# Three banks in rotation for transposes and PV, scores of the heads apart in quarter one, norm weights folded into the rounding

## The chip, the cores and the metric

The kernel runs on one core of a Trainium2 chip. The metric is the device time of one execution in microseconds (us), median of three runs. The core has these engines: PE or TensorE (matrix products and transposes), DVE or VectorE, ACT or ScalarE, POOL or GpSimd, and SP, which here only issues transfers. Each works through its own queue in order. Products land in PSUM, eight banks of 128 partitions by 512 float32 values.

## The reference

One layer of a transformer trunk in float32: 2048 tokens, width 1024, 16 heads of 64, a feed-forward of width 2816. With depth 1 it is:

```
h = rms_norm(x, g_pre_mix)
q, k, v = heads of h @ w_qkv
for chunk c (64 queries): keys of chunks max(0, c-8) .. c
    p = softmax(q @ k.T / 8 + bias[relative position, clipped])
    o = p @ v
x = x + rms_norm(o @ w_o, g_post_mix)
h = rms_norm(x, g_pre_ffn)
x = x + rms_norm((silu(h @ w_gate) * (h @ w_up)) @ w_down, g_post_ffn)
```

rms_norm divides by the root of the mean square of a token and multiplies by a weight for each column.

## The kernel before

**Products.** A float32 product is made of rounded parts: an operand is split into a high part (rounded by ScalarE) and a low part (the rest, a VectorE subtraction; `split`, L352). `products` (L195) makes three matmuls of it, high by high, high by low, low by high (L197, L198, L199). The large products of the projections and of the feed-forward also work on sums and differences of quarter matrices in the way of Strassen, so an operand comes in columns named B11, B21, T1, T2, B22, T4, T3. `Blocks.build` makes these columns from four raw loads (L11, L21, L12, L22), and `put` splits each.

**Order.** TensorE runs its instructions in program order (a manual schedule, L1509). The other engines' instructions are ordered by the compiler's scheduler. Work that is not TensorE's main line stands in a queue `later` as pairs (cost, step); `tick(w)` is called with each triple of matmuls (a unit, some 0.68 us), and it runs steps as their costs are covered. `pause(w)` is a step that only waits; `timed` sets steps to given units.

**Stages.** First the projections: `project` (L1277) goes through two groups of 1024 tokens. In each, values come first (`values_of`), then queries and keys (`queries_keys`), with one product for each column name; after each, a callback `after(name)` queues the columns of group two into buffers that have become free. The roots of the norms come through `roots` and `roots_by_tokens` (L1311), whose argument `back` is the pause before the root is spread. Group one ends at about 275 us, group two at about 498.

Then attention, in four quarters of 512 tokens in the order n = 1, 0, 2, 3 (`SEQ_OF`), each with 8 jobs (two heads by 512 queries) of four steps (128 queries each). The step, in program order:

```
[each fourth step: half the fill, then output() of the job before]
job.transposed(t % 4)          # head 0: 4 transposes, DVE copy L551; head 1: 4, ACT copy L553
scaled() of step t + 2         # DVE reciprocal L530, POOL scaling L533
scores of step t + 3           # 8 matmuls L508, L509; per head DVE L517 (bias, minimum), ACT exp L521
[each fourth step: low(), the DVE subtraction L585 that reads po]
half the fill
job.fifth()                    # 2 transposes L562, ACT copy L563
half the fill
```

`output` (L584) is PV, 32 matmuls into one bank (16 to 20 for n = 0), an ACT eviction L584 and the subtraction `low`. The fill is the output projection of the quarter before (`o_quarter`), so quarter one has none. For n = 0 there are fewer key blocks and no fifth. PSUM: `st`, one tile of three banks, holds the scores of both heads; for n = 0 head 0 stands in its first bank and head 1 in its second (`cuts`, `(0, n), (512, 512 + n)`), else the heads follow each other and share the middle bank. `tt` has two buffers of one bank, `po` one bank, and the pool `ps` two (tag `mm`) for the fill and the rest.

After the attention the last output projection (1103 to 1145 us) runs while the feed-forward's first columns are loaded and built (`first`, L1630 on), and then the feed-forward to the end.

Of the kernel before, what the change touches and what calls it, by code (L numbers as in the profile page):

```python
# [49 lines left out]
def trunk(  # L50
# [393 lines left out]

    class Attend:


        def __init__(self, n, p):
            self.n, self.p = n, p
            self.prev = n > 0  # L450
            self.sc = {}
            self.pT = None

# [37 lines left out]
        def scores(self, ib):  # L491
# [9 lines left out]
            if "S" not in phase:  # L501
                phase["S"] = phase["psa"].tile([P, 3 * HALF], F32, name="st", bufs=1)
            st = phase["S"]
# [33 lines left out]
        def transposed(self, ib):  # L537
# [6 lines left out]
            for h in range(2):  # L544
                part = blocks[:4]
                tt = phase["psa"].tile([P, 4, P], F32, tag="tt", name="tt", bufs=2)
                for u, (r, b) in enumerate(part):
                    pe.transpose(tt[:, u, :], sc[h][:, b * P : b * P + P], ident)  # L548
                dst = self.pT[:, h, 0 : len(part), cols]
                if h == 0:  # L550
                    dve.tensor_copy(dst, tt[:, : len(part), :])  # L551
                else:
                    act.activation(dst, tt[:, : len(part), :], AF.Copy)  # L553
            self.rest = (sc, blocks[4], cols) if self.prev else None

        def fifth(self):
            if self.rest is None:
                return
            sc, (r, b), cols = self.rest
            tt = phase["psa"].tile([P, 4, P], F32, tag="tt", name="tt", bufs=2)  # L560
            for h in range(2):
                pe.transpose(tt[:, h, :], sc[h][:, b * P : b * P + P], ident)  # L562
            act.activation(self.pT[:, :, 4, cols], tt[:, 0:2, :], AF.Copy)  # L563

        def output(self):
# [8 lines left out]
            po = phase["psa"].tile([P, HALF], F32, tag="po", name="po", bufs=1)  # L574
# [36 lines left out]
    class Blocks:  # L611
# [53 lines left out]
        def put(self, name, k, src):  # L665
            if name not in self.t:
                self.t[name] = hb_tile(self.slot[name])
            split(self.t[name][:, 0, k, :], self.t[name][:, 1, k, :], src)

        def build(self, part, w, prep):  # L670
# [17 lines left out]

            def b11(k):
                prep(0, k, at("T3", 1, k))  # L690
                self.put("B11", k, at("T3", 1, k))

            def b21(k):
                prep(0, k + 4, at("T4", 1, k))
                self.put("B21", k, at("T4", 1, k))

            def t1(k):
# [3 lines left out]
                self.put("T1", k, a)  # L701

            def t2(k):
# [3 lines left out]
                dve.tensor_tensor(a, c, a, op=ALU.add)  # L707
                self.put("T2", k, a)
                dve.tensor_tensor(b, b, c, op=ALU.subtract)
                dve.tensor_tensor(a, d, a, op=ALU.subtract)  # L710
# [566 lines left out]
    def project():  # L1277

        warm = ps.tile([P, HALF], F32, tag="mm", name="warm")
        for _ in range(28):  # L1280
# [7 lines left out]
        def prepare(g):  # L1288
            def prep(t, k, x_):
# [4 lines left out]
                act.activation(x_, x_, AF.Copy, scale=gt[:, PRE_MIX, k : k + 1])  # L1294
# [3 lines left out]
        def build(g, part, w=0.0):  # L1298
            return groups[g].build(part, w, prepare(g))
# [48 lines left out]
        for k, (_, f) in enumerate(build(0, "B11")):  # L1348
# [6 lines left out]
            (1.0, build(0, "B21", 2.5)), (14.0, build(0, "T1", 3.5)[:1]), (17.0, roots(0, 2.0)),  # L1355
            (20.0, build(0, "T1", 3.0)[1:]), (30.0, build(0, "T2", 3.5)), (45.0, roots_by_tokens(1, 0.5, 2.0, spare)),
# [3 lines left out]
        for g in range(NG):  # L1360
# [7 lines left out]
            def after(name, g=g):  # L1368
# [10 lines left out]
                elif name == "T2":  # L1379
                    later.extend(timed((0.5, build(1, "B21", 1.8))))  # L1380
                elif name == "B22":
                    later.extend(timed((0.5, build(1, "T1", 1.8))))
                elif name == "T3":
                    later.extend(timed((0.5, build(1, "T2", 3.0))))
                elif name == "T4":
                    later.extend(timed(
                        (20.0, build(1, "B22", 3.0)), (34.0, build(1, "T4", 3.0)), (50.0, build(1, "T3", 2.0)),
# [206 lines left out]
    for part in ("L11", "L21", "L12", "L22"):  # L1594
        first(part, 0.0)[0][1]()
    later.extend(blocks[0].spreads() + timed(
# [80 lines left out]
```

## Time and profile before

| | |
|---|---|
| median of 3 runs | 2446.71 us (2444.43 to 2447.67) |
| profiled execution | 2446.41 us |
| its span | 2444.6 us |
| TensorE busy | 2347.2 us, 96% |
| VectorE, ScalarE, GpSimd busy | 1644.1, 1163.2, 316.7 us |
| mean granted TensorE clock | 0.991 of full speed |

The rows of the profile are read as: start and length, or busy time, then engine, line (L12 is line 12 of the kernel), operation, output and input by the program's names, shapes, and in square brackets how long the engine stood idle before and what released it. PEld is TensorE's weight load. Matmul lengths overlap in the pipeline, so distances between starts are used for what a matmul costs.

### The profile page before, as it was taken

Reading aid. Unit: us, or ns where it says so; the run is one execution under the profiler, and the core shown is the slowest. Engines: PE = TensorE matmul, PEld = TensorE weight load, DVE = VectorE, ACT = ScalarE, POOL = GpSimd, SP = SyncE. Lnnn points to the kernel's source line nnn. Section 1 sums busy time; section 2 is a strip of 40 time slices with the busy share of each in tenths; the row PEclk is TensorE's granted clock in tenths of the full one; section 3 lists DMA queues with packets and bytes.
Section 4 is the critical chain, followed back from the end, with each engine's and each line's share of the span. In section 5 each row is a group of like instructions: output and inputs, shape, how many; then the busy total and the mean of one; then the engine's idle time right before and its main releaser. Section 6 shows DMA issues by size and latency. Waiting matters only on the chain.

```text
span 2444.6 us, 33016 instructions
## 1 busy us (share of the span) xinstructions
PE 2347.2 (96%) x11480; PEld 1903.1 (78%) x11480; DVE 1644.1 (67%) x2625; ACT 1163.2 (48%) x2039; POOL 316.7 (13%) x422
## 2 busy tenths in 40 slices
PE   8999899989999899998999999999999999999998
PEld 6887688866676676767887888888888888888887
DVE  7775856666665556667876777677657667555567
ACT  8443733357665555664433333365433333334454
POOL 1012110023334324330000000000000000000002
PEclk9999999999999999999999999999999999999999
DMA  7699997678798878946666544287666757446654
GB/s 281 215 293 311 306 274 233 186 208 226 198 230 234 261 207 227 246 139 235 230 210 238 194 173 167 101 268 240 213 219 202 235 158 239 137 169 233 193 187 153
DMA packets 229782, 529.72 MB, mean 217 GB/s; under 512 B 26320, under 2 KB 42720, under 8 KB 225136
## 3 DMA queue, kind: packets, MB, share of 16 engines
q1 hardware_dynamic: 217712, 480.42, 62.6%
q0 software_dynamic: 11904, 47.19, 6.5%
q8 instruction: 91, 1.49, 0.3%
q14 instruction: 75, 0.61, 0.1%
HBM read 380.14 MB, written 170.44 MB: 225 GB/s over the span
## 4 chain that ended last, share of the span: by engine, by line
PE 54%; DVE 2%; issue 2%; DMA 1%; ACT 1%; POOL 0%; SPq 0%; DVEq 0%; ACTq 0%; POOLq 0%
PE pd L199 6%; PE pd L198 6%; PE pd L197 6%; PE pb L197 4%; PE pb L199 4%; PE pb L198 4%; PE pc L199 3%; PE pc L198 3%; PE pc L197 3%; PE pa L198 3%; PE pa L199 3%; PE pa L197 3%; PE po L578 1%; PE mm L199 1%; PE mm L197 1%
## 5 line engine op out<-in xcount | busy, mean ns | idle before, releaser
L533 POOL TENSOR_SCALAR sc<-sc,rows 128x640 f32<-128x640 f32 (+4 forms) x256 | 195.6, 777 | 364.7 <-DVE rows L530 221.9
L521 ACT ACTIVATE sc<-sc,rows 128x640 f32<-128x640 f32 (+4 forms) x256 | 192.9, 755 | 88.6 <-DVE rows L517 88.1
L517 DVE CUSTOM_DVE_ANT_0 sc<-st,bias 128x640 f32<-128x640 f32 (+2 forms) x248 | 173.6, 734 | 57.0 <-PE st L509 31.9
L197 PE MATMUL pb<-hb,w_wg_T 128*128 128x512 f32 x528 | 206.4, 391 | 3.8 <-DVE terms L966 3.8
L199 PE MATMUL pb<-hb,w_wg_T 128*128 128x512 f32 x528 | 206.2, 391 | 0.0
L198 PE MATMUL pb<-hb,w_wg_T 128*128 128x512 f32 x528 | 206.1, 390 | 0.0
L548 PE MATMUL tt<-ident,sc 128*128 128x128 f32 x928 | 135.0, 278 | 34.3 <-DVE pT L551 10.2
L548 PEld LDWEIGHTS tt<-ident,sc 128*128 128x128 f32 x928 | 105.1, 141 | 76.9 <-issue 45.0
L508 PE MATMUL st<-k,q 128*128 128x384 f32 (+3 forms) x432 | 137.4, 338 | 14.4 <-DVE rows L517 13.1
L199 PE MATMUL pd<-a,w_d_T 128*128 128x512 f32 (+1 forms) x368 | 139.9, 380 | 0.1
L197 PE MATMUL pd<-a,w_d_T 128*128 128x512 f32 (+1 forms) x368 | 139.9, 380 | 0.0
L198 PE MATMUL pd<-a,w_d_T 128*128 128x512 f32 (+1 forms) x368 | 139.8, 380 | 0.0
L551 DVE COPY pT<-tt 128x512 f32<-128x512 f32 (+3 forms) x128 | 81.5, 637 | 83.7 <-PE tt L548 63.6
L198 PE MATMUL pa<-hb,w_wg_B 128*128 128x512 f32 x352 | 136.9, 389 | 0.0
L197 PE MATMUL pa<-hb,w_wg_B 128*128 128x512 f32 x352 | 136.9, 389 | 0.0
L199 PE MATMUL pa<-hb,w_wg_B 128*128 128x512 f32 x352 | 136.9, 389 | 0.0
L968 ACT ACTIVATE terms<-terms 128x512 f32<-128x512 f32 x65 | 41.1, 632 | 182.5 <-DVE terms L966 182.5
L131 ACT ACTIVATE w_wg_T<-raw 128x1024 fp32r<-128x1024 f32 x88 | 92.9, 1057 | 71.9 <-PE pa L199 35.1
L509 PE MATMUL st<-k,q 128*128 128x384 f32 (+3 forms) x432 | 126.9, 314 | 0.0
L354 DVE TENSOR_TENSOR a<-raw_a,a 128x512 fp32r<-128x512 f32 x154 | 105.5, 692 | 25.2 <-ACT a L353 24.8
L289 POOL TENSOR_TENSOR rs<-ms,neg_half 128x4 f32<-128x4 f32 (+1 forms) x7 | 8.4, 1201 | 863.9 <-DVE ms L287 863.9
L197 PEld LDWEIGHTS pb<-hb,w_wg_T 128*128 128x128 f32 x528 | 99.5, 188 | 25.8 <-issue 4.6
(265 smaller groups left out, 6248.9 us busy)
## 6 DMA issues: line engine op xcount, KB each, us to landing
raw<-in_w_gu SPq DMA_DIRECT2D x77, 512.0 KB, 4.2
q<-q SPq DMA_DIRECT2D x62, 512.0 KB, 6.7
k<-k SPq DMA_DIRECT2D x54, 512.0 KB, 9.0
s_g_S<-raw POOLq DMA_DIRECT2D x44, 512.0 KB, 3.0
raw_d<-d_S SPq DMA_DIRECT2D x88, 256.0 KB, 3.6
raw_a<-aT SPq DMA_DIRECT2D x88, 256.0 KB, 3.5
raw<-s_g_S SPq DMA_DIRECT2D x44, 512.0 KB, 4.2
bias<-ext_d SPq DMA_DIRECT2D x124, 144.0 KB, 9.0
```

What stands on the lines that cost most here:

```text
L131: act.activation(hi, raw, AF.Copy)
L197: pe.matmul(pt, a_hi, b_hi, start=first, stop=False, skip_group_check=go_on)
L198: pe.matmul(pt, a_hi, b_lo, start=False, stop=False, skip_group_check=go_on)
L199: pe.matmul(pt, a_lo, b_hi, start=False, stop=last, skip_group_check=go_on)
L354: eng.tensor_tensor(lo, src, hi.bitcast(F32), op=ALU.subtract)
L508: pe.matmul(st[:, a:b], q[:, 2 * h, cols], kk[:, h, key], start=True, stop=False)
L509: pe.matmul(st[:, a:b], q[:, 2 * h + 1, cols], kk[:, h, key], start=False, stop=True)
L517: dve.tensor_tensor_reduce(out=sc[:, :n], in0=st[:, c0 : c0 + n], in1=rev, scale=-1.0, scalar=3.0e38, op0=ALU.add, op1=ALU.min, accum_out= ...
L521: act.activation(sc[:, :n], sc[:, :n], AF.Exp, bias=nmax, scale=-1.0, accum_out=rows[:, h : h + 1])
L533: last_pool[0] = pool.tensor_scalar(sc[:, :n], sc[:, :n], rows[:, 2 + h : 3 + h], 1.0, op0=ALU.mult, op1=ALU.mult)
L548: pe.transpose(tt[:, u, :], sc[h][:, b * P : b * P + P], ident)
L551: dve.tensor_copy(dst, tt[:, : len(part), :])
```

## The change

Attention: one PSUM tile of six banks, `banks`, takes the place of `st`, `tt` and `po`. In quarters two to four the scores keep banks 0 to 2, and transposes, fifth transposes and PV take banks 3, 4, 5 in turn. In quarter one (`alone`) head 0's scores stand in banks 0 and 1, head 1's in 2 and 3, the fifth in 4, PV in 5, and the first transposes in the two `mm` buffers of the pool `ps`, which no fill uses there.

Projections: `prepare` no longer multiplies each raw column by the norm weight on ScalarE. With `lazy`, `put` gives the weight as scale to the rounding (ScalarE) and to the subtraction (VectorE); T2's two other results take it in their VectorE operation, and one of its inputs by a ScalarE copy. In B11 and B21 the square for the norm's sum comes after the split. The warm-up matmuls go from 28 to 20, the pauses before the spreads of roots 0 and 1 from 2 to 14 and from 2 to 8 units. Group two's B21 columns are queued after B22 rather than T2, and T1 and T2 after T4, with the later ones set back.

Feed-forward: `fetch()`, which issues the loads of the next weights, is called after the first of four raw loads.

```
--- before.py
+++ after.py
@@ -442,14 +442,33 @@
             for h, own in enumerate(heads):
                 sp.dma_start(k_d[n][p][heads[a], h, :], part[own])
 
+    turn_of = [0]
+
+    def banks():
+        if "banks" not in phase:
+            phase["banks"] = phase["psa"].tile([P, 6 * HALF], F32, name="banks", bufs=1)
+        return phase["banks"]
+
     class Attend:
 
 
         def __init__(self, n, p):
             self.n, self.p = n, p
             self.prev = n > 0
+            self.alone = n == SEQ_OF[0]
             self.sc = {}
             self.pT = None
+
+        def bank(self, name):
+
+            if self.alone and name != "t5":
+                return ps.tile([P, HALF], F32, tag="mm", name="tt")
+            if self.alone:
+                at = 4
+            else:
+                at = 3 + turn_of[0] % 3
+                turn_of[0] += 1
+            return banks()[:, at * HALF : at * HALF + HALF]
 
         def load(self, begin=False):
             n, p, ap = self.n, self.p, phase.get("ap")
@@ -498,9 +517,9 @@
             else:
                 n, k0 = (ib + 1) * P, HALF
                 cuts = [(0, n), (512, 512 + n)]
-            if "S" not in phase:
-                phase["S"] = phase["psa"].tile([P, 3 * HALF], F32, name="st", bufs=1)
-            st = phase["S"]
+            st = banks()
+            if self.alone:
+                cuts = [(0, 512, 640), (1024, 1536, 1664)]
             for h in range(2):
                 c0 = cuts[h][0]
                 for a, b in zip(cuts[h][:-1], cuts[h][1:]):
@@ -543,7 +562,7 @@
             blocks = self.blocks(ib)
             for h in range(2):
                 part = blocks[:4]
-                tt = phase["psa"].tile([P, 4, P], F32, tag="tt", name="tt", bufs=2)
+                tt = self.bank("tt").rearrange("p (a b) -> p a b", a=4)
                 for u, (r, b) in enumerate(part):
                     pe.transpose(tt[:, u, :], sc[h][:, b * P : b * P + P], ident)
                 dst = self.pT[:, h, 0 : len(part), cols]
@@ -557,7 +576,7 @@
             if self.rest is None:
                 return
             sc, (r, b), cols = self.rest
-            tt = phase["psa"].tile([P, 4, P], F32, tag="tt", name="tt", bufs=2)
+            tt = self.bank("t5").rearrange("p (a b) -> p a b", a=4)
             for h in range(2):
                 pe.transpose(tt[:, h, :], sc[h][:, b * P : b * P + P], ident)
             act.activation(self.pT[:, :, 4, cols], tt[:, 0:2, :], AF.Copy)
@@ -571,7 +590,7 @@
                     terms.append((r, r - 1, 0, r * P))
                 if r < 4:
                     terms.append((r, 4 + r, r * P, HALF))
-            po = phase["psa"].tile([P, HALF], F32, tag="po", name="po", bufs=1)
+            po = banks()[:, 5 * HALF : 6 * HALF] if self.alone else self.bank("po")
             for m, (r, kb, c0, c1) in enumerate(terms):
                 for h in range(2):
                     c = (p % 2) * P + h * 64
@@ -662,12 +681,17 @@
                 dst, dst, gt[:, self.gain, k : k + 1], self.rows[t], op0=ALU.mult, op1=ALU.mult
             )
 
-        def put(self, name, k, src):
+        def put(self, name, k, src, scale=None):
             if name not in self.t:
                 self.t[name] = hb_tile(self.slot[name])
-            split(self.t[name][:, 0, k, :], self.t[name][:, 1, k, :], src)
-
-        def build(self, part, w, prep):
+            hi, lo = (self.t[name][:, n, k, :] for n in range(2))
+            if scale is None:
+                split(hi, lo, src)
+                return
+            act.activation(hi, src, AF.Copy, scale=scale)
+            dve.scalar_tensor_tensor(lo, src, scale, hi.bitcast(F32), op0=ALU.mult, op1=ALU.subtract)
+
+        def build(self, part, w, prep, lazy=False):
 
 
             def raw(name, half, t, k0, each=1):
@@ -686,28 +710,45 @@
             if part[:3] in loads:
                 return [(w, raw(*loads[part[:3]], 1 if part[3:] else 4))]
 
+            def gain(k):
+                return gt[:, self.gain, k : k + 1] if lazy else None
+
+            def joined(out, one, k, other, op):
+                if lazy:
+                    dve.scalar_tensor_tensor(out, one, gain(k), other, op0=ALU.mult, op1=op)
+                else:
+                    dve.tensor_tensor(out, one, other, op=op)
+
             def b11(k):
-                prep(0, k, at("T3", 1, k))
-                self.put("B11", k, at("T3", 1, k))
+                if not lazy:
+                    prep(0, k, at("T3", 1, k))
+                self.put("B11", k, at("T3", 1, k), gain(k))
+                if lazy:
+                    prep(0, k, at("T3", 1, k))
 
             def b21(k):
-                prep(0, k + 4, at("T4", 1, k))
-                self.put("B21", k, at("T4", 1, k))
+                if not lazy:
+                    prep(0, k + 4, at("T4", 1, k))
+                self.put("B21", k, at("T4", 1, k), gain(k + 4))
+                if lazy:
+                    prep(0, k + 4, at("T4", 1, k))
 
             def t1(k):
                 a, b = at("T3", 1, k), at("T3", 0, k)
                 prep(1, k, b)
                 dve.tensor_tensor(a, a, b, op=ALU.subtract)
-                self.put("T1", k, a)
+                self.put("T1", k, a, gain(k))
 
             def t2(k):
                 a, b = at("T3", 1, k), at("T3", 0, k)
                 c, d = at("T4", 0, k), at("T4", 1, k)
                 prep(1, k + 4, c)
-                dve.tensor_tensor(a, c, a, op=ALU.add)
+                if lazy:
+                    act.activation(c, c, AF.Copy, scale=gain(k + 4))
+                joined(a, a, k, c, ALU.add)
                 self.put("T2", k, a)
-                dve.tensor_tensor(b, b, c, op=ALU.subtract)
-                dve.tensor_tensor(a, d, a, op=ALU.subtract)
+                joined(b, b, k, c, ALU.subtract)
+                joined(a, d, k + 4, a, ALU.subtract)
 
             def b22(k):
                 self.put("B22", k, at("T4", 0, k))
@@ -1277,7 +1318,7 @@
     def project():
 
         warm = ps.tile([P, HALF], F32, tag="mm", name="warm")
-        for _ in range(28):
+        for _ in range(20):
             pe.matmul(warm[:, 0:P], ident, ident, start=True, stop=True)
         groups = [Blocks([x[2 * g + t] for t in range(2)], PRE_MIX, SLOTS[g]) for g in range(NG)]
         for g in range(NG):
@@ -1291,12 +1332,11 @@
                     totals[0] = phase["fp"].tile([P, HALF], F32, tag="tot", name="total", bufs=2)
                 if g == t == 0:
                     add_square(x_, totals[0], k == 0)
-                act.activation(x_, x_, AF.Copy, scale=gt[:, PRE_MIX, k : k + 1])
 
             return prep
 
         def build(g, part, w=0.0):
-            return groups[g].build(part, w, prepare(g))
+            return groups[g].build(part, w, prepare(g), True)
 
         def now(steps):
             for _, f in steps:
@@ -1352,8 +1392,8 @@
         big = xp.tile([P, 10, HALF], F32, tag="big", name="terms", bufs=1)
         spare = big[:, 8:10, :].rearrange("p a c -> p (a c)")
         later.extend(timed(
-            (1.0, build(0, "B21", 2.5)), (14.0, build(0, "T1", 3.5)[:1]), (17.0, roots(0, 2.0)),
-            (20.0, build(0, "T1", 3.0)[1:]), (30.0, build(0, "T2", 3.5)), (45.0, roots_by_tokens(1, 0.5, 2.0, spare)),
+            (1.0, build(0, "B21", 2.5)), (14.0, build(0, "T1", 3.5)[:1]), (17.0, roots(0, 14.0)),
+            (20.0, build(0, "T1", 3.0)[1:]), (30.0, build(0, "T2", 3.5)), (45.0, roots_by_tokens(1, 0.5, 8.0, spare)),
             (52.0, build(0, "B22", 2.0)), (62.0, build(0, "T4", 2.0)), (71.0, build(0, "T3", 1.0)),
             (100.0, [(0.0, bias_rows)]),
         ))
@@ -1376,15 +1416,12 @@
                     now(build(1, "L21") + build(1, "L22"))
                 elif name == "T1":
                     later.extend(timed((0.5, build(1, "B11", 1.8))))
-                elif name == "T2":
+                elif name == "B22":
                     later.extend(timed((0.5, build(1, "B21", 1.8))))
-                elif name == "B22":
-                    later.extend(timed((0.5, build(1, "T1", 1.8))))
-                elif name == "T3":
-                    later.extend(timed((0.5, build(1, "T2", 3.0))))
                 elif name == "T4":
                     later.extend(timed(
-                        (20.0, build(1, "B22", 3.0)), (34.0, build(1, "T4", 3.0)), (50.0, build(1, "T3", 2.0)),
+                        (1.0, build(1, "T1", 2.5)), (14.0, build(1, "T2", 4.0)), (31.0, build(1, "B22", 3.0)),
+                        (44.0, build(1, "T4", 3.0)), (57.0, build(1, "T3", 2.0)),
                     ))
 
             yield from queries_keys(g, groups[g], big, after)
@@ -1593,6 +1630,8 @@
     first = lambda part, w: blocks[0].build(part, w, lambda t, k, x_: blocks[0].norm(x_, t, k))
     for part in ("L11", "L21", "L12", "L22"):
         first(part, 0.0)[0][1]()
+        if part == "L11":
+            fetch()
     later.extend(blocks[0].spreads() + timed(
         (3.0, first("B11", 2.5)), (15.0, first("B21", 2.5)), (28.0, first("T1", 4.0))
     ))
```

## The prediction

> **What bounds the kernel now.** I read the page first (busy shares, the slices, the chain), then a table of busy time by stage, then the waits of TensorE, then short timelines inside the attention.
>
> ```profile
> span 2444.6 us, 33016 instructions
> PE 2347.2 (96%) x11480; PEld 1903.1 (78%) x11480; DVE 1644.1 (67%) x2625; ACT 1163.2 (48%) x2039; POOL 316.7 (13%) x422
> ...
> PE 54%; DVE 2%; issue 2%; DMA 1%; ACT 1%; POOL 0%; SPq 0%; DVEq 0%; ACTq 0%; POOLq 0%
> ```
>
> TensorE is busy 96% of the span and heads the chain. The profiled execution took 2446.41 us, its span and 1.8 around it; the median of the runs is 2446.71, so sums below start from 2446.4. What can be won is only TensorE's idle and slow time, and the table by stage says where that lies:
>
> ```profile
> 20.00:40.00 20.00, 14.33 (x59) 11.36 (x58) 18.08 (x23) 18.95 (x33) 5.07 (x8) 0.84 0.84 333
> 240.00:300.00 60.00, 52.17 (x216) 41.45 (x215) 50.88 (x76) 45.10 (x74) 6.19 (x8) 0.94 0.94 299
> 545.00:655.00 110.00, 100.62 (x679) 72.85 (x677) 68.80 (x179) 74.56 (x175) 39.60 (x56) 1.00 0.78 207
> 747.00:925.00 178.00, 160.24 (x1026) 123.74 (x1024) 106.72 (x227) 105.58 (x230) 67.54 (x75) 0.99 0.83 232
> 1330.00:2400.00 1070.00, 1069.16 (x4720) 884.27 (x4719) 713.66 (x986) 430.31 (x650) 21.41 (x29) 1.00 0.59 196
> ```
>
> The columns are length, then PE, PEld, DVE, ACT and POOL busy, the granted clock and the DMA share. The feed-forward stage (last row) has nothing to win; the start, the border between the two groups of the projections and the attention quarters have some. The waits give the sizes:
>
> ```profile
> PE st L508 <- DVE rows L517: 18.1, 31, 3.3
> PE tt L548 <- DVE pT L551: 10.2, 11, 1.4
> PE tt L548 <- DVE rows L530: 8.6, 7, 2.5
> PE tt L548 <- ACT pT L563: 7.7, 11, 1.1
> PE prs L349 <- POOL hr L289: 5.5, 1, 5.5
> PE pb L197 <- ACT hi L435: 4.5, 1, 4.5
> PE mm L197 <- ACT w L131: 3.2, 1, 3.2
> PE mm L199 <- DVE w L132: 2.3, 1, 2.3
> ```
>
> The change aims at all of these: the first four (44.6 us) with the banks, the fifth and sixth with the projections' schedule, the last two with fetch().
>
> **Banks: what a shared tile costs.** Before, scores (`st`), transposes (`tt`) and the output product (`po`) are separate PSUM tiles. After, all of them (but quarter one's first transposes) are slices of one six-bank tile, `banks`. Everything hangs on whether accesses to different banks of one tile wait for each other. The quarter with n = 0 shows that already, for there head 0's scores lie in bank 0 of `st` and head 1's in bank 1:
>
> ```profile
> 643.48 0.40 PE L509 MATMUL st<-k,q 128*128 128x512 f32 x1
> 643.72 0.69 DVE L585 TENSOR_TENSOR hb<-po,hb 128x512 fp32r<-128x512 f32 x1
> 643.95 0.40 PE L509 MATMUL st<-k,q 128*128 128x512 f32 x1
> 644.50 0.69 DVE L517 CUSTOM_DVE_ANT_0 sc<-st,bias 128x512 f32<-128x512 f32 x1
> 645.12 0.69 DVE L517 CUSTOM_DVE_ANT_0 sc<-st,bias 128x512 f32<-128x512 f32 x1
> 645.86 0.33 PE L508 MATMUL st<-k,q 128*128 128x128 f32 x1 [1.07 <-DVE rows L517]
> ```
>
> Head 0's bank is complete at 643.88 and VectorE comes free at 644.41, yet its read starts at 644.50, 0.15 after head 1's last matmul (643.95 + 0.40). In the other direction, head 0's bank has been read by 645.19, but TensorE's next score into it stands still for 1.07 and starts at 645.86, just after the read of head 1's bank (645.81). So the program orders accesses to one tile as a whole, a write behind reads of other banks and a read behind writes to them. If that holds for `banks`, scores, transposes, PV and their evictions run strictly one after another in program order, across three engines. I take this as the likeliest, since the rows are of this kernel and of this very kind of slice.
>
> Price in quarters three and four, from one step and one PV row:
>
> ```profile
> 899.84 0.60 PE L548 MATMUL tt<-ident,sc 128*128 128x128 f32 x4
> 900.47 0.69 DVE L551 COPY pT<-tt 128x512 f32<-128x512 f32 x1 [0.38 <-PE tt L548]
> 901.31 0.63 PE L548 MATMUL tt<-ident,sc 128*128 128x128 f32 x4 [0.88 <-DVE pT L551]
> 902.24 0.60 ACT L553 ACTIVATE pT<-tt 128x512 f32<-128x512 f32 x1
> ...
> 904.68 4.53 PE L578 MATMUL po<-pT,v 128*64 128x512 f32 x32
> ```
>
> ```profile
> 549.77 0.45 PE L508 MATMUL st<-k,q 128*128 128x384 f32 x1 [0.37 <-DVE rows L517]
> 551.05 0.38 PE L562 MATMUL tt<-ident,sc 128*128 128x128 f32 x2
> 551.47 0.38 ACT L563 ACTIVATE pT<-tt 128x256 f32<-128x256 f32 x1 [0.25 <-PE tt L562]
> 552.98 0.44 PE L508 MATMUL st<-k,q 128*128 128x384 f32 x1 [0.35 <-DVE rows L517]
> 553.04 0.81 ACT L521 ACTIVATE sc<-sc,rows 128x640 f32<-128x640 f32 x1
> ```
>
> Head 0's transposes to head 1's through the copy: 1.47 (899.84 to 901.31; today this wait comes in some steps, then in all). Head 1's transposes, ScalarE's copy, a hand-over: 0.63 + 0.60 + 0.14 = 1.37 until the scores. Scores and both reads until TensorE may write again: 3.21 (549.77 to 552.98, the loop of quarter one, which is this very chain). Fifth transposes (551.05 to 551.47) and their copy until the next step's: 0.42 + 0.38 + 0.14 = 0.94, or 1.4 where the copy queues behind the second exp, which starts only 0.06 after TensorE goes on (553.04, 0.81 long). A step is 7.0 to 7.45. The output projection's fill, 192 matmuls in a quarter by 0.227 (4720 in 1069.16 in the table's last row), 0.68 in a half step, hides under the reads and the last copy. PV adds 4.46 (32 matmuls, 0.14 a piece), its ScalarE eviction before the next transposes (0.60 as the copy at 902.24, and hand-overs of some 0.25), and the later subtraction L585, 0.69, which the fifth transposes now wait for. A job is four steps and that: 34.0 to 35.8. Today it is 178 / 8 = 22.2 by the table. That is +11.8 to 13.6 for 16 jobs, +189 to 218; I take 203.
>
> ```profile
> 541.26 4.53 PE L578 MATMUL po<-pT,hb 128*64 128x512 f32 x32
> 624.51 4.53 PE L578 MATMUL po<-pT,v 128*64 128x512 f32 x32
> 654.05 2.38 PE L578 MATMUL po<-pT,v 128*64 128x512 f32 x16
> 733.04 2.38 PE L578 MATMUL po<-pT,v 128*64 128x512 f32 x16
> ```
>
> Quarter one (five jobs between the first two rows, 16.65 each) keeps its first transposes in other tiles, so they run beside the chain: 3.21 and the fifth with its copy, 0.9 to 1.5, is 4.1 to 4.75 a step (I take 4.6, since nothing there moves the copy ahead of the exp), with PV 5.4 and L585 0.6: 24.4 a job, +7.75 by 8 = +62 (45 to 67). Heads apart brings nothing here, as n = 0 shows. Quarter two (six jobs between the other two rows, 13.17 each) has no fifth, and its steps have one to four key blocks. The rows above cut to the mean of 2.5 blocks, an estimate, are 0.45 and 0.47 for head 0's transposes and copy, 0.45 and 0.45 for head 1's, 0.7 for scores, 1.0 for both reads; with four hand-overs of 0.14 a step is 4.1. PV here takes 2.38, with evictions 3.8: a job is 4 x 4.1 + 3.8 = 20.2, +56 (45 to 62). Attention: +321, between 279 and 347.
>
> **The rest of the change, taken together: -23 (-13 to -30).**
>
> ```profile
> 260.86 0.63 PE L198 MATMUL pb<-hb,w_wq_T 128*128 128x512 f32 x1
> 1099.51 2.02 SPq L72 DMA_DIRECT2D hb<-x  x4
> 1101.57 1.13 SPq L72 DMA_DIRECT2D raw<-in_w_o  x2
> 1125.11 0.63 PE L198 MATMUL mm<-hb,w 128*128 128x512 f32 x1
> ```
>
> After each of the long waits in the list (5.5, 4.5, 3.2 and 2.3) matmuls take 0.63 instead of the 0.40 seen above, at the lower granted clock, some 16 of them at 0.2 too much: 3.4 on top. Start: putting the roots 12 units (some 8 us) later ends the 5.5 and that tail, but VectorE is busy 18.08 of 20 us there and becomes the limit, so I take 7 of 8.9 (4 to 10). Folding the norm weight into the rounding removes 12 of 16 ScalarE copies (some 0.6 each) a group and adds four scaled ones; VectorE's count stays. Eight warm matmuls fewer count for at most 2 inside that. Border: T1 and T2 of group two (some 20 VectorE passes of 0.69) leave a stretch where VectorE works 50.88 of 60 and move behind T4 into the next values (over the span VectorE is busy 67%, so a third is free); of 4.5 + 3.4 and small waits I take 8 (5 to 11). If that cover fails, T2 comes late for its product and up to 5 of it returns. Entry to the feed-forward: fetch() moves on SP's queue ahead of three of the four loads of x that stand before its weights today (1099.51, 1101.57); I take these to land early enough for the 3.2 and 2.3 to go, with the clock's tail 8 (6 to 9). What is put back are the L21, L12 and L22 loads, by some 4 us, with no TensorE wait near their use today.
>
> **Two rules beside these rows.** The Trainium skill, "PSUM — Partial Sum Buffer", section "PSUM bank collisions raise a hardware error", asks for order only between engines on one bank and quadrant and reports pairs on different banks clean; by it the edit gives the time of the first rival. The rows of n = 0 disagree, as the program waits across banks, and they decide. "TensorE: Matmul & The Clock Gate" in the Trainium skill, section "HAM oscillation — how this bites in real kernels", warns of idle gaps over some 3.4 us; the trace agrees (0.63 after waits of 3.2 to 5.5).
>
> **The sum.** 2446.4 + 321 - 23 = 2744, call it 2743. Its own range, from the ends above and some disorder on the queues of ScalarE and VectorE, is 2640 to 2850.
>
> **Rivals.**
> - Banks are independent (other side: faster). For it: the edit's rotation and split of heads make sense only so. Against it: the 0.15 and the 1.07 above. Of the 44.6 of waits the reciprocal's 8.6 stays in half: 40 gone, with 23 elsewhere: 2383. It decides as soon as a read of one bank starts while another is written.
> - Banks are independent but the third bank doesn't help: TensorE then waits for reciprocal and scaling instead, 20 of the 40 stay: 2403. For it: the L530 row, 8.6 already.
> - The serial chain and the lower clock together. Gaps there reach 1.9 (3.21 less the 1.28 from 549.77 to 551.05), while the slow matmuls followed waits of 3.2 and more; a wait of 1.07 was followed by none. If the clock still fell in the whole attention, TensorE's share of a step (0.60 + 0.63 + 1.28 + 0.38 = 2.9) and PV (4.46) would double, 16 a job: 16 x 16 = 256 in quarters three and four, and with 11 and 7 a job in one and two, 144 more, +400. From a quarter of the steps to all, that is 2840 to 3140.
> - The change does little: gains elsewhere eaten by a part of the order, 2441 to 2451.
>
> **Chances.** Serial chain 0.77, with the low clock 0.06, independent banks 0.11, with the reciprocal's wait 0.04, little 0.02. Runs of one kernel lie within 0.2%, some 5 us, which is what a measurement tells apart. So faster 0.15, same 0.02, slower 0.83. The range 2580 to 2930 holds the first case and the lower part of the second; the faster rivals are outside it.
>
> **What would show it.** Right: waits of tt L548, st L508 and tt L562 for evictions in every step of quarters two to four, a PV distance of about 35, each copy beginning after TensorE stopped; TensorE near 60% there, at full clock. The start's 5.5, the border's 4.5 and the entry's 3.2 gone. Wrong: if VectorE reads head 0's scores while head 1's are written, the order is by bank and the first rival holds.

## The result and the profile after

The changed kernel takes 2864.84 us (median of four runs, 2859.17 to 2866.65) against 2445.83 for the kernel before in the same comparison: a ratio of 1.1709, with an interval from 1.1688 to 1.1729. It is 419 us slower; 2743 was forecast, with a range of 2580 to 2930.

The page of the changed kernel, its span, the busy shares and the clock in 40 slices of 71.6 us:

```profile
span 2862.4 us, 33164 instructions
PE 2512.2 (88%) x11464; PEld 1977.0 (69%) x11464; DVE 1651.3 (58%) x2625; ACT 1157.8 (40%) x2015; POOL 314.7 (11%) x422
...
PEclk9999999776799799979999999999999999999999
```

TensorE is busy for 165 us more, though it has the same work and eight warm-up matmuls less: part of it ran at a lower clock. The lowest digits stand in slices 8 to 18, all in the attention, which fills slices 8 to 22. The table by stretches has the columns of the table before (length, PE, PEld, DVE, ACT, POOL, clock, DMA share, GB/s):

```profile
20.00:40.00 20.00, 19.88 (x93) 15.94 (x91) 19.89 (x26) 16.07 (x25) 4.48 (x7) 1.00 0.90 344
...
240.00:300.00 60.00, 54.30 (x229) 44.42 (x228) 54.33 (x79) 37.32 (x60) 7.73 (x10) 0.94 0.99 315
550.00:750.00 200.00, 142.85 (x683) 101.22 (x682) 68.71 (x173) 74.18 (x173) 41.01 (x56) 0.73 0.40 104
750.00:860.00 110.00, 81.19 (x363) 54.64 (x361) 39.43 (x121) 41.16 (x109) 19.93 (x36) 0.87 0.46 123
860.00:1157.00 297.00, 202.65 (x985) 139.82 (x985) 108.78 (x248) 105.50 (x237) 66.25 (x79) 0.89 0.48 139
1157.00:1500.00 343.00, 230.90 (x1175) 155.55 (x1173) 125.72 (x263) 125.92 (x269) 72.21 (x82) 0.90 0.43 125
1560.00:2800.00 1240.00, 1235.70 (x5464) 1021.74 (x5463) 850.87 (x1167) 497.98 (x743) 28.19 (x47) 1.00 0.61 202
```

In the four rows from 550 to 1500, the attention, no engine is full: TensorE is busy for about 70% of the time, VectorE and ScalarE for little over a third. That is how a chain across engines looks. TensorE's waits name its links:

```profile
PE banks L581 <- DVE rows L536: 84.0, 68, 1.9
PE banks L527 <- ACT pT L572: 59.4, 93, 1.2
PE banks L567 <- DVE pT L570: 51.1, 59, 2.1
PE banks L581 <- DVE hb L604: 41.2, 23, 2.7
PE banks L567 <- POOL sc L552: 29.6, 32, 1.0
PE banks L567 <- ACT hb L603: 19.3, 24, 1.0
...
PE pb L197 <- DVE terms L1290: 8.0, 2, 5.7
```

In the new lines, L567 are the transposes, L581 the fifth ones, L527 the scores. The fifth transposes wait for VectorE's reading of scores (84.0), scores wait for ScalarE's copy of transposes (59.4), the second head's transposes for VectorE's copy of the first's (51.1), and so on. The two sides of each of these three pairs stand in different banks. TensorE in one step of quarter three:

```profile
1050.06 0.63 PE L567 MATMUL banks<-ident,sc 128*128 128x128 f32 x4 [0.79 <-ACT hb L603]
1051.62 0.63 PE L567 MATMUL banks<-ident,sc 128*128 128x128 f32 x4 [0.93 <-DVE pT L570]
1052.94 0.69 PE L527 MATMUL banks<-k,q 128*128 128x384 f32 x1 [0.69 <-ACT pT L572]
...
1057.85 0.44 PE L581 MATMUL banks<-ident,sc 128*128 128x128 f32 x2 [1.49 <-DVE hb L604]
```

And a step of quarter one, where the heads' scores lie apart, TensorE and VectorE:

```profile
601.88 0.27 PE L528 MATMUL banks<-k,q 128*128 128x128 f32 x1
...
602.56 0.28 PE L528 MATMUL banks<-k,q 128*128 128x128 f32 x1
603.07 0.82 DVE L536 CUSTOM_DVE_ANT_0 sc<-banks,bias 128x640 f32<-128x640 f32 x1 [2.04 <-PE banks L528]
603.82 0.82 DVE L536 CUSTOM_DVE_ANT_0 sc<-banks,bias 128x640 f32<-128x640 f32 x1
604.70 0.44 PE L581 MATMUL banks<-ident,sc 128*128 128x128 f32 x2 [1.86 <-DVE rows L536]
...
606.87 0.63 PE L528 MATMUL banks<-k,q 128*128 128x512 f32 x1
```

Head 0's scores are complete at 602.15 and VectorE has been idle for 2.04, yet it reads them at 603.07, after head 1's last matmul (602.84). Both rows of the n = 0 quarter come back, now between all users of `banks`. The 0.63 in the last row is new: a matmul of 512 columns at the lower clock, after a wait of only 1.86.

Where the 418 us of span went, by the first score and the last PV of each trace: the first score comes 9.5 earlier (489.2 for 498.7), from there to the start of the last PV it is 438.0 longer (1038.6 for 600.6), and behind it 10.7 shorter (1334.5 for 1345.2). The expectations below have 8.9 and 437, taken from a score 0.6 later.

### The profile page after: what moved, and what is told of

It is laid out like the page before. It is cut to its first block, busy times and chain, and to the rows that moved or that the text cites. A ratio compares the mean times of both kernels' runs of the same rounds, so it can differ in the third digit from the quotient of the medians.

```text
span 2862.4 us, 33164 instructions
## 1 busy us (share of the span) xinstructions
PE 2512.2 (88%) x11464; PEld 1977.0 (69%) x11464; DVE 1651.3 (58%) x2625; ACT 1157.8 (40%) x2015; POOL 314.7 (11%) x422
## 3 DMA queue, kind: packets, MB, share of 16 engines
q8 instruction: 91, 1.49, 0.2%
## 4 chain that ended last, share of the span: by engine, by line
PE 56%; ACT 5%; DVE 5%; issue 3%; DMA 2%; POOL 2%; SPq 0%; DVEq 0%; POOLq 0%; ACTq 0%
PE pd L199 5%; PE pd L197 5%; PE pd L198 5%; PE pb L197 4%; PE pb L199 4%; PE pb L198 4%; PE banks L597 3%; PE banks L567 3%; PE banks L527 3%; PE pa L197 3%; ACT sc L540 3%; PE pa L199 3%; PE pa L198 3%; PE pc L197 3%; PE pc L199 3%; PE pc L198 3%
## 5 line engine op out<-in xcount | busy, mean ns | idle before, releaser
L536 DVE CUSTOM_DVE_ANT_0 sc<-banks,bias 128x640 f32<-128x640 f32 (+2 forms) x248 | 173.3, 736 | 322.4 <-PE banks L528 306.4
L527 PE MATMUL banks<-k,q 128*128 128x384 f32 (+3 forms) x432 | 173.6, 412 | 59.4 <-ACT pT L572 59.4
L567 PE MATMUL banks<-ident,sc 128*128 128x128 f32 x672 | 116.4, 292 | 120.2 <-DVE pT L570 51.1
L567 PEld LDWEIGHTS banks<-ident,sc 128*128 128x128 f32 x672 | 77.3, 148 | 179.0 <-issue 104.8
L527 PEld LDWEIGHTS banks<-k,q 128*128 128x128 f32 x432 | 103.5, 240 | 88.6 <-ACT pT L572 82.4
L581 PE MATMUL banks<-ident,sc 128*128 128x128 f32 x192 | 48.1, 338 | 125.9 <-DVE rows L536 84.0
L528 PE MATMUL banks<-k,q 128*128 128x384 f32 (+3 forms) x432 | 156.6, 385 | 0.0
L570 DVE COPY pT<-banks 128x512 f32<-128x512 f32 (+2 forms) x96 | 59.9, 624 | 154.1 <-PE banks L567 151.1
L597 PE MATMUL banks<-pT,v 128*64 128x512 f32 (+3 forms) x832 | 131.7, 472 | 8.6 <-ACT pT L582 5.9
L581 PEld LDWEIGHTS banks<-ident,sc 128*128 128x128 f32 x192 | 21.8, 158 | 162.1 <-DVE rows L536 110.1
L572 ACT ACTIVATE pT<-banks 128x512 f32<-128x512 f32 (+2 forms) x96 | 52.2, 543 | 192.5 <-PE banks L567 192.5
```

Source lines behind the costliest of these rows:

```text
L527: pe.matmul(st[:, a:b], q[:, 2 * h, cols], kk[:, h, key], start=True, stop=False)
L528: pe.matmul(st[:, a:b], q[:, 2 * h + 1, cols], kk[:, h, key], start=False, stop=True)
L536: dve.tensor_tensor_reduce(out=sc[:, :n], in0=st[:, c0 : c0 + n], in1=rev, scale=-1.0, scalar=3.0e38, op0=ALU.add, op1=ALU.min, accum_out= ...
L597: pe.matmul(po[heads[h], c0:c1], v[:, kb, c : c + 64], self.pT[:, h, r, c0:c1], start=m == 0, stop=m == len(terms) - 1,)
```

## Experiments

| kernel | time | ratio to before, interval | PV distance, quarters 1 to 4 |
|---|---|---|---|
| changed kernel | 2864.84 | 1.1709 (1.1688 to 1.1729) | 30.8, 22.8, 38.0, 37.3 |
| banks_only | 2885.45 | 1.1795 (1.1764 to 1.1827) | 30.7, 22.8, 37.6, 37.9 |
| own_tiles | 2414.27 | 0.9864 (0.9840 to 0.9888) | 16.6, 13.2, 21.7, 21.9 |
| turn_tile | 2610.12 | 1.0668 (1.0642 to 1.0693) | 17.1, 17.5, 31.7, 32.2 |
| apart_one | 2474.19 | 1.0113 (1.0098 to 1.0128) | 17.3, 13.9, 24.7, 26.2 |
| apart_two | 2454.27 | 1.0031 (1.0019 to 1.0043) | 16.0, 13.8, 24.1, 25.3 |
| apart_switch | 2406.01 | 0.9840 (0.9821 to 0.9860) | 16.0, 13.2, 21.7, 22.1 |
| later_sum | 2400.75 | 0.9824 (0.9811 to 0.9838) | 16.0, 13.2, 21.8, 20.1 |
| busy_q1 | 2826.12 | 1.1553 (1.1519 to 1.1586) | 25.3, 23.2, 37.5, 37.4 |
| busy_half | 2827.03 | 1.1539 (1.1490 to 1.1587) | 25.3, 22.6, 38.6, 37.3 |
| no_banks | 2432.03 | 0.9945 (0.9924 to 0.9966) | 16.6, 13.2, 22.4, 23.6 |
| no_group2 | 2430.33 | 0.9944 (0.9927 to 0.9960) | 16.6, 13.2, 22.4, 22.5 |
| fetch_only | 2435.77 | 0.9966 (0.9953 to 0.9979) | 16.6, 13.2, 22.5, 22.8 |

The distances are means over six jobs of each quarter, between starts of their first PV matmul; before they are 16.6, 13.2, 22.8 and 22.8.

**Which part is it: banks_only and no_banks.** The diff cut in two: `bank`, `banks` and their uses, or all the rest.

> The kernel before with the attention's part of the change alone. Theory: all of the loss and more, 2446 + 437 = 2883 (2870 to 2895), clock in quarter one some 0.73. Rival (the loss needs the other edits too, their deferred work on VectorE and ScalarE falling into the attention): under 2800.

> The kernel before with all of the change but the attention: weights folded into the rounding, pauses, 20 warm matmuls, group two's schedule, fetch(). Theory: these gain what the two traces show outside the attention, 8.9 until the first score and 10.7 behind the last PV, so 2427 (2422 to 2432). Rival: the later first score is bought by work put off into the attention, which the serial chain hid; then 2436 to 2446.

Banks alone cost everything and more, 2885.45, as the theory had it (2883). The rest alone gains: 2432.03, at the upper end of what was expected. So the 20.2 that the traces show outside the attention are not all kept.

**The tile or the banks: own_tiles.**

```
-    return banks()[:, at * HALF : at * HALF + HALF]      # one tile of six banks
+    return phase["psa"].tile([P, HALF], F32, tag="turn", name=name, bufs=3)
...
-    cuts = [(0, 512, 640), (1024, 1536, 1664)]           # quarter one: as before
```

> The changed kernel, but scores are a PSUM tile of three banks of their own (heads behind each other, as before), and transposes, fifths and PV take turns over three separate tiles of one bank each: the same rotation over three banks, no shared tile. Theory (the program orders all accesses to one tile, whatever the bank): the serial waits go, PV starts come back to 16.5, 13 and 22 us apart or less, the granted clock to 0.99, and the time to 2400, between 2385 and 2430 (2426 if the rotation brings nothing over two buffers and one). Rival (the engines disturb each other in PSUM when transposes, scores and PV rotate, whatever tiles they stand in): the time stays above 2600.

The same number of banks in turn, with tiles of their own, takes 2414.27, 451 less than the changed kernel and 33 less than before. TensorE's larger waits in the attention are then those of the scores (L520 scores, L529 VectorE's reading, largely in quarter one) and one of 7.2 for a sum of the feed-forward's norm (L282), with none left on transposes:

```profile
PE st L520 <- DVE rows L529: 26.9, 31, 3.3
PE pb L197 <- DVE terms L1283: 9.7, 3, 5.0
PE pssq L282 <- DVE total L265: 8.4, 2, 7.2
PE st L520 <- DMA k<-k: 5.8, 5, 3.3
```

The rival, engines disturbing each other in PSUM, falls. It also shows what the third bank is worth once nothing else is in the way: the three lines of `tt` waits of before (26.5) are gone. Beside no_banks, which has the rest of the change and takes 2432.03, that is some 18 us; a part of the 26.5 comes back as other waits, those for scores, for instance, at 26.9 where no_banks has 19.4.

**Do heads apart help: apart_one and apart_two.** Head 0 in banks 0 and 1, head 1 in 2 and 3; the two kernels differ in this alone:

```
-    st = phase["psa"].tile([P, 4 * HALF], ...)                               # apart_one
+    sts = [phase["psa"].tile([P, 2 * HALF], ..., tag=f"st{h}") for h in range(2)]   # apart_two
```

> As own_tiles, but the heads' scores stand apart in all quarters, head 0 in banks 0 and 1, head 1 in banks 2 and 3 of one four-bank tile; transposes, fifths and PV take turns over the two banks left. Control for apart_two. Theory (a tile is one unit for the order): heads apart brings nothing, quarter one's PV distance stays 16.6, and two banks in turn rather than three cost something in the later quarters: 2414 to 2445. Rival (order by bank): quarter one falls to about 14.5, as in apart_two.

> The same banks and the same places as apart_one, but the two heads' scores are two tiles of two banks each. Nothing else differs. Theory: VectorE reads head 0 while head 1 is written, TensorE's waits on the scores (0.67 each in quarter one) go, its step falls from 3.21 to its own work of some 2.85, quarter one's PV distance to about 15, and the whole is 12 to 20 under apart_one. Rival (order by bank or by address already): no difference between the two.

One tile, 2474.19; two tiles in the same places, 2454.27: 20 less, as expected. In apart_two VectorE (L531) and TensorE (L522, L523) overlap:

```profile
550.47 0.39 PE L523 MATMUL st<-k,q 128*128 128x512 f32 x1
550.52 0.81 DVE L531 CUSTOM_DVE_ANT_0 sc<-st,bias 128x640 f32<-128x640 f32 x1
550.76 0.28 PE L523 MATMUL st<-k,q 128*128 128x128 f32 x1
...
551.26 0.82 DVE L531 CUSTOM_DVE_ANT_0 sc<-st,bias 128x640 f32<-128x640 f32 x1
551.90 0.48 PE L522 MATMUL st<-k,q 128*128 128x512 f32 x1
```

Head 0 is read from 550.52, while head 1's matmuls run to 551.04, and the next score of head 0 starts at 551.90, while head 1 is read. Some sizes missed. apart_one is 29 over the range: two banks for transposes, fifths and PV are worse than before's two and one, at 24.7 to 26.2 in quarters three and four. Quarter one's distance is 17.3 in apart_one rather than 16.6, and in apart_two it falls to 16.0 only, not 15. The waits on scores, apart_one first, and then apart_two with its busy times in a stretch of quarter one:

```profile
PE st L520 <- DVE rows L529: 23.3, 28, 3.2
```

```profile
PE st L522 <- DVE rows L531: 2.6, 2, 2.4
```

```profile
560.00:640.00 80.00, 77.28 (x510) 59.35 (x510) 48.07 (x134) 51.84 (x131) 30.51 (x44) 1.00 0.78 211
```

They are all but gone, and TensorE works 97% of the stretch, so 16.0 is its own work at full clock; the step of 2.85 was put too low.

**The layout as described, with tiles: apart_switch and later_sum.** In quarter one two score tiles of two banks and two single banks; at the first score of quarter two that pool is closed and one with a tile of three banks and three singles opened.

> The layout that the change describes, with tiles of their own: in quarter one two tiles of two banks for the heads and two single banks in turn for fifth and PV, then one tile of three banks for scores and three single banks in turn. Theory: quarter one as in apart_two (PV distance about 15), the others as in own_tiles: 2397, between 2388 and 2405. Rival (the change of layout between quarters one and two waits for everything before it): not under 2410.

> As apart_switch, but in quarter four the column sums of the feed-forward's first norm go to TensorE 12 units after their last load's step rather than 3. In apart_switch TensorE stands 7.2 there, at 1022, for a VectorE sum whose load is late. Theory: the wait is TensorE's own and goes: 2399 (2394 to 2403). Rival (the load is late however long it is waited for, or the norm's row then comes late for the feed-forward): 2404 or more.

2406.01, between theory and rival and a microsecond over the range: the distances are those of apart_two and own_tiles, but other things now come late, the transfers of k (8.9) and a sum for a norm (7.2):

```profile
PE st L529 <- DVE rows L538: 9.4, 10, 2.4
PE st L529 <- DMA k<-k: 8.9, 6, 3.1
PE pssq L282 <- DVE total L265: 7.2, 1, 7.2
```

later_sum, with `steps.append((12.0,` for `(3.0,` in `sums`, takes 2400.75. The 7.2 has become 2.7; the two intervals overlap, so the 5 between the two times (4 by the ratios) are likely rather than shown. Both beat the kernel before and the changed one.

**How the loss divides: turn_tile.** own_tiles with its three single banks as slices of one three-bank tile.

> As own_tiles, but the three banks in turn are one tile of three banks; scores have their own. It tells which part of the six-bank tile costs what. Theory: transposes, fifths and PV with their evictions run one after another, scores don't: some 0.9 more in each step of quarters three and four (PV distance 25 to 26), 0.6 and an eviction more in quarter two (16 to 17), next to nothing in quarter one: 2500, between 2470 and 2540, so that sharing with the scores makes over three quarters of the loss. Rival (the transposes' turn carries the loss): over 2650.

A miss: 2610.12. Sharing among transposes, fifths and PV makes 196 of the 451 between own_tiles and the changed kernel; sharing with the scores, and the slower clock that comes with it (0.941 on the mean, against 0.981 in turn_tile), the rest, 255, not over three quarters. TensorE's waits in turn_tile name what my step left out (L564 transposes, L579 the fifth's copy):

```profile
PE turn L564 <- DVE pT L567: 50.5, 57, 2.1
PE turn L564 <- ACT pT L579: 46.0, 32, 2.2
PE turn L564 <- POOL sc L549: 35.1, 37, 1.4
PE turn L594 <- ACT pT L579: 20.6, 23, 1.7
```

Transposes wait 1.4 on the mean for the fifth's copy (46.0 in 32 waits), and PV 0.9 (20.6 in 23). ScalarE's queue has the exps of both heads ahead of that copy, so although scores have their own tile, their eviction is in the chain again.

**The clock: busy_q1 and busy_half.** Eight, or four, extra matmuls of 128 columns ahead of the fifth transposes in quarter one of the changed kernel:

```
+    w = ps.tile([P, HALF], F32, tag="mm", name="warm")
+    for _ in range(8):                    # busy_half: 4
+        pe.matmul(w[:, 0:P], ident, ident, start=True, stop=True)
```

> The changed kernel with eight extra 128x128 float32 matmuls, results unused, ahead of the fifth transposes of quarter one, where TensorE stands 1.86 in each step. At full clock they take 1.9. Theory (the clock falls because TensorE works too small a share of the time, though no single gap is over 2.7): with the gap filled quarter one's clock rises from 0.73 to over 0.95 and its PV distance falls from 30.7 to some 25, so the whole to some 2820, with more work. Rival (the clock falls for another reason): it stays at 0.73, the extra work takes 3 us a step instead of 1.9, and the time rises to 2890 or more.

> As busy_q1, but with four extra matmuls in each step of quarter one instead of eight, so that half of the gap of 1.9 stays and the step gets no longer at full clock. Theory (the clock follows the share of time that TensorE works; 0.73 without, 0.99 with eight): four leave gaps of 0.9, as the quarter one of before has them nearly (0.6 at full clock), so the clock comes back to over 0.9, the PV distance to 25 to 27, the whole to 2815 to 2835. Rival (it needs the gap filled whole): clock under 0.85, PV distance over 28, the whole 2845 or more.

The same stretch of quarter one in the changed kernel, in busy_half and in busy_q1, in this order:

```profile
530.00:700.00 170.00, 122.31 (x587) 89.33 (x584) 62.00 (x143) 65.59 (x143) 34.13 (x44) 0.73 0.44 117
```

```profile
530.00:700.00 170.00, 135.84 (x924) 103.00 (x925) 73.36 (x178) 78.25 (x177) 43.13 (x56) 0.97 0.49 130
```

```profile
530.00:700.00 170.00, 156.50 (x1134) 125.82 (x1133) 71.30 (x174) 77.43 (x175) 43.13 (x56) 0.99 0.49 130
```

More work made quarter one faster: 25.3 for 30.8 a job, by 8 jobs 44 us, and the whole came down by 39. So in quarter one the clock fell because TensorE stood idle for so much of each step, and half of the filling suffices; in the other quarters this was not tried. The Trainium skill, "TensorE: Matmul & The Clock Gate", section "HAM oscillation — how this bites in real kernels", gives idle gaps over some 3.4 us as what to avoid. Here gaps of 1.9 in every 6 us, none over 2.7, brought a mean clock of 0.73. In quarters three and four of the changed kernel the waits are shorter, 0.6 to 1.6 on the mean in the larger groups and 2.4 at most, and the clock was 0.89 and 0.90. In quarter two, in a stretch without a wait over 0.9, it was still 0.92:

```profile
765.00:901.00 136.00, 99.17 (x464) 67.39 (x463) 53.08 (x160) 53.98 (x143) 25.90 (x48) 0.92 0.56 151
```

So no single long gap is needed. The share of busy time in the rows is no measure by itself, about 70% in all four quarters, since a slower clock stretches busy time. Taken times the clock it is 0.52 of the time in quarter one, 0.61 in three and four, 0.67 in quarter two and 0.78 in busy_half, in the order of their clocks. But that product holds the clock that it is to explain, and length and share of the gaps were not varied apart. What the clock follows stays open.

**The rest: no_group2 and fetch_only.** no_banks without the hunk of `after`; and before with `fetch()` after L11 alone.

> As no_banks, but group two's columns keep their times from before. It prices that edit alone, 2432 being the time with it. Theory (the border's wait only changes its cause, from the rounding of a column to the products' sums on VectorE, which is full there): the edit is worth 3, this takes 2435 (2431 to 2438). Rival (as forecast: the schedule is worth 8): 2440 or more.

> The kernel before with fetch() after the first raw load, nothing else of the change. Theory: the waits of 3.2 and 2.3 and the slow matmuls behind them go, about 9 to 11 of the 15 that no_banks gained: 2437 (2434 to 2440). Rival (the transfer is late anyway): 2445 to 2449.

fetch_only gains 9 of the 15 (2435.77), as expected. no_group2 takes 2430.33, neither what the theory nor what the rival gave: at 0.9944 against 0.9945 group two's schedule has no measurable worth. Its border wait is on the products' sums on VectorE in either case, and none is left on the rounding (4.5 before), so it is not the schedule that removed that one; the folding of the norm weight, which both kernels have, is the likely reason. First no_banks, then no_group2:

```profile
PE pb L197 <- DVE terms L1271: 6.8, 2, 3.9
```

```profile
PE pb L197 <- DVE terms L1271: 9.3, 2, 6.4
```

The schedule does bring the first score forward, 488.6 for 494.0, but the two spans are 2429.0 and 2427.8, so those 5.4 are gone again by the end. One profile each can't tell whether that is the schedule's doing: no_banks has a single wait of 4.7 on GpSimd's `y` in quarter four that no_group2 lacks.

## Why the prediction was right, and where its terms were off

**The mechanism.** "The program orders accesses to one tile as a whole" decided sign and size, and came from two rows of the kernel before, of two banks of one tile. own_tiles and the pair apart_one and apart_two show it as the cause. The Trainium skill's page "PSUM — Partial Sum Buffer", section "PSUM bank collisions raise a hardware error", which reports two engines on different banks as clean, is not contradicted: in apart_two engines work on different banks at the same time. The order is in the program, per tile, not in the memory. The pool of these tiles is opened with `reuse_waits="tile"` in all the kernels; whether the order within a tile depends on that option was not tried.

**Attention: +321 forecast, +438 measured.** Per job 24.4, 20.2 and 34.9 were forecast and 30.8, 22.8 and some 37.7 measured. The failed term is the clock, which the sum put at full. "Gaps there reach 1.9, while the slow matmuls followed waits of 3.2 and more" was the reason to give the lower clock 0.06; it fell to 0.73, 0.87, 0.89 and 0.90. The reason also passed over a row of the kernel before. There a wait of 2.48, the longest of the L530 line that the prediction shows, was followed by matmuls of 0.63 at half the clock:

```profile
811.39 0.63 PE L548 MATMUL tt<-ident,sc 128*128 128x128 f32 x4 [2.48 <-DVE rows L530]
...
813.87 0.63 PE L197 MATMUL mm<-hb,w 128*128 128x512 f32 x1
```

```profile
812.00:815.40 3.40, 3.40 (x14) 3.00 (x13) 2.28 (x4) 0.60 (x1) 3.40 (x3) 0.50 1.03 255
```

So slow matmuls followed a gap of 2.5 already, and the prediction's "the trace agrees" claimed too much.

At nearly full clock quarter one takes 25.3 (busy_q1, busy_half), 0.9 over its forecast, so the clock's part there is the 44 above. For the others an estimate from the table: a mean clock c over a busy time b means b x (1 - c) lost, 81.19 x 0.13 = 11, 202.65 x 0.11 = 22 and 230.90 x 0.10 = 23. With the 44 of quarter one that is 100 of the 117 by which the attention missed. So the forecast's first case and its rival of the chain with the lower clock came together, but with the clock down for a part of the time, 100 rather than 400.

The stated range held for that reason and not by the sum: 2864.84 lies above the first case's own 2640 to 2850, and in the 2840 to 3140 of the case that was given 0.06. The sign and the chain were foreseen with their reason; the size was covered by a case held unlikely. Of the signs, "TensorE near 60% there, at full clock" failed in its clock; taken times the clock, the busy share is 61% in quarters three and four, as forecast.

**The step.** Its links measured: 1.56 from transposes to transposes (forecast 1.47), 1.32 to the scores (1.37), and the fifth held by L585's new line L604, 1.49 beyond the fill. The wait of the fifth's copy behind the second exp was in the chain at up to 0.5; the changed kernel's next transposes wait for that copy 23 times, 10.0 in all, some 0.4 each, while turn_tile, where the scores have a tile of their own, shows 1.4 on the mean of 32 waits.

**The rest: -23 forecast, -15 alone (no_banks).** fetch(): 8 forecast, 9 measured. Start and border together: 15 forecast, some 5 to 6 kept. The start's own waits (5.5, and its slow matmuls) are gone, the clock in 20 to 40 is 1.00 for 0.84. The mis-sized term is the border, 8: the wait of 4.5 on the rounding is gone, but the waits on VectorE's sums, which the kernel before has there too, have grown. The line of before, beside the 8.0 and 5.7 of L1290 above:

```profile
PE pb L197 <- DVE terms L1249: 3.8, 2, 2.2
```

All of TensorE's waits between 200 and 300 us come to 10.1 before, 8.0 in the changed kernel and 6.8 in no_banks. That is 2 to 3 won, or 5 to 6 by the 13.0 of fetch_only, whose projections are those of before; one profile each tells it no closer. That VectorE is too full is the likely reason, not shown: it is busy 54.33 of 60 in the border's row, more than the 50.88 before. The forecast named T2's columns as what could come late there, not the sums.

**The rivals.** Independent banks (2383) is what tiles of their own approach: 2400.75 in later_sum, with transfers of k (10.4) and the border (9.0) in the way. That is next to the 2403 of the second rival, but not for its reason, for no wait of the transposes on the reciprocal is left.

## What to carry to other kernels

Slices of one PSUM tile are not a way to give engines separate banks: where the program orders by tile, every user waits for every other, so give each bank that is to be independent a tile of its own, and open a new pool where the layout changes. Before a layout is built on the assumption that two areas are independent, look in the trace for a place where two such areas exist already, and whether a reader starts before the writer of the other ends. When a chain makes TensorE idle for a good part of each step, add a slower clock to the price, since the waits bring it on and it lengthens the work between them: here it made some 100 of 438 us.

## What had not been expected of the hardware

The granted clock fell to 0.73 with waits of at most 2.7 us, 1.9 as a rule, repeated every step; in the kernel before, the waits ahead of slow matmuls were 2.5 to 5.5. Even a stretch of the changed kernel whose longest wait was 0.9 had 0.92. Adding matmuls whose results nobody uses, some 2.0 us in a step for eight and 1.1 for four, brought it back to 0.97 with four in a step and to 0.99 with eight, and took 38 to 39 us off the whole.
